# Hybrid encoder trunk: the second chunk of tokens prepared step by step in every group

## Chip, cores and metric

The kernel runs on one core of a Trainium2 chip. The metric is the device time of one execution in microseconds (us). Before the change it is 2895.91 us, the median of 3 runs (2895.25 to 2896.24).

## What is computed

One layer of a streaming encoder works on 2048 prompt tokens and on 8 x 16 sample tokens, with a model width of 1024:

```
h = RMSNorm(x);  p = h @ w_in            (1024 x 9216, split in column segments)
A: gated short convolution    B: gated linear recurrence, 4 heads    C: stick-breaking attention, 8 heads
y_x = o_x @ w_branch[rows of x]          for x in A, B, C
out = x + (sigmoid(m_a) y_a + sigmoid(m_b) y_b + sigmoid(m_c) y_c) @ w_out
```

Besides the result, the last rows of the convolution, the recurrent states and the keys and values are outputs.

## The kernel before, in words

The tokens are 17 tiles of 128 (tile 0 holds the sample tokens). `GROUPS` (L39) puts them into three groups of two chunks: [0,1,2] and [3,4]; [5,6,7] and [8,9,10]; [11,12,13] and [14,15,16]. For each group, `run_jobs` (L1317) walks over some 70 jobs. A job is one slice of weight columns, and a *turn* is one job on one chunk. `order` (L1327 to L1330) lists the turns of a group; in groups 1 and 2 it begins with (job 0, chunk 0), (job 1, chunk 0), (job 0, chunk 1), (job 1, chunk 1), numbered `at_` = 0 to 3. Jobs 0 and 1 of groups 1 and 2 are gate slices of the attention branch (`sz_job`, L1178): 24 matmuls of 128x384 each (`proj_chan`, L704, matmul at L710), with a `yield` after every 6. Products are made from split operands (high part and remainder), three passes each.

Between two yields of a turn, `run_jobs` issues other work: late post-processing, the recurrence (`hbg`), and background work (`bg`). The background work is the attention over the cached keys of the sample tokens in group 1, and the prompt attention (`attn_pair`, L297) in group 2 and in the merge stage behind it. The prompt attention begins in group 2's turn 0: it loads Q, K and V tiles (L281, L282, L287, L291), forms scores on TensorE (L329, L330), two sigmoids on ScalarE (L333, L335), masks on GpSimd (L338), a scan and a product on VectorE (L342, L347), and transposes on TensorE (L310) that a ScalarE copy evicts (L311).

`Prepare` (L585) turns x tiles into what the matmuls read, in steps:

- `load` (L598): a DMA of 512 KB into an `xt` tile (L607, on the SP queue), the sum of squares on ScalarE (L614), then two small operations on GpSimd (L232, L234).
- `scale` (L617): one operation on VectorE (L619).
- `turn` (L621), twice per tile: four transposes on TensorE (L629) into a PSUM tile `tp` (two buffers, shared with the attention and the sample attention), then a cast on ScalarE (L175) and a subtraction on VectorE (L176) into `hx`.

For groups 1 and 2 the order of the steps is written in `steps` (L633):

```
for i in range(n):
    for kk in range(0, KB, 4): self.turn(i, kk); yield
    for k in [i + 2] if self.final and i == 3 else [] if self.final and i == 2 else [i + 3]:
        if k < n: self.load(k); yield
    if i + 2 >= 3 and i + 2 < n: self.scale(i + 2); yield
    self.ready = i
```

There are three `xt` buffers: two in the pool `xp`, one in `xq`, and in the last group `xq` is used for tile index 2 alone (`room`, L602). So there the DMA of tile index 5 needs the buffer of index 3.

The next group's `Prepare` is begun in the last five turns of a group (L1350, L1359). `prep.chunk(ci)` (L687) runs all steps that are still missing until chunk `ci` is complete. It is called at each turn (L1348) for that turn's chunk. At the call for chunk 0 the generator stops behind the first `turn` of tile index 3; the others of chunk 1 are issued at once by the call of `at_` = 2. In group 1 these are six steps: turn(3,4), scale(5), turn(4,0), turn(4,4), turn(5,0), turn(5,4). In group 2 they are seven, with load(5) behind turn(3,4). In group 0 another list of steps (`first_steps`) is advanced in turns 0 and 1, two steps at each yield (L1356).

The framework that builds the kernel gives each engine its instruction order: it takes what is ready in its own model of time, and of that what stands first in the program. On the chip each engine then runs its list in that order.

Of the kernel before, what the change touches and what calls it, by code (L numbers as in the profile page):

```python
# [98 lines left out]
def trunk(ctx: ExitStack, tc: tile.TileContext, x_prompt, x_sample, cache_conv, state_hgrn, cache_k, cache_v,  # L99
# [88 lines left out]
    def wload(pieces, key):  # L188


        out = []
        for n, v in enumerate(pieces):
            a, b = v.shape[1], v.shape[2]
            if (key, n) in kept:
                turns[0] += 1
                if turns[0] % 4 == 0:

                    hl = []
                    for i in range(2):
                        x = wp.tile([P, a, b], F32, tag="wst", name="wst", bufs=2)  # L200
                        nc.sync.dma_start(x, kept[key, n][:, i].rearrange("p (a b) -> p a b", a=a).bitcast(F32))
                        hl.append(x.bitcast(F32R))
                    out.append((*hl, None))
                    continue
            w = wp.tile([P, 2, 1024], F32R, tag="w", name="w")
            hi, lo = (w[:, i].rearrange("p (a b) -> p a b", a=a) for i in range(2))
            if (key, n) in kept:
                nc.sync.dma_start(w.bitcast(F32), kept[key, n].bitcast(F32))
            else:
                st = wp.tile([P, a, b], F32, tag="wst", name="wst", bufs=2)  # L210
                nc.sync.dma_start(st, v)
                with ExitStack() as order:
                    if len(kept) < 1 and n:

                        for x in prep.last:
                            order.enter_context(tc.issue_after(x.ins))
                    split(hi, lo, st)
            out.append((hi, lo, w))
        return out
# [527 lines left out]
    def build_vectors():  # L747
        nc.sync.dma_start(qg_bc, q_norm_g[0].partition_broadcast(P))
        nc.sync.dma_start(kg_bc, k_norm_g[0].partition_broadcast(P))

        vrow = g0p.tile([17, P], F32, tag="mtmp", name="vrow", bufs=2)
        nc.sync.dma_start(vrow[0:12], conv_w[0].rearrange("j (b p) -> (j b) p", p=P))
        nc.sync.dma_start(vrow[12:16], hg_lb_logits[0].rearrange("(h p) -> h p", p=P))
        nc.sync.dma_start(vrow[16:17], hg_norm_g)
        pvec = ps_tp()
        nc.tensor.transpose(pvec[:, 0:17], vrow, idf[0:17, 0:17])
        nc.vector.tensor_copy(vec, pvec[:, 0:17])
# [10 lines left out]
    def build_bound():  # L768
        lmax = const.tile([P, 4], F32, name="lmax")
        nc.vector.tensor_copy(lmax, vec[:, 12:16])  # L770
        lexp = const.tile([P, 4], F32, name="lexp")
        nc.vector.tensor_tensor(lexp, vec[:, 12:16], lmax, ALU.subtract)
        ebase = const.tile([P, 1], F32, name="ebase")
        nc.vector.memset(ebase, 2.718281828459045)
        nc.gpsimd.tensor_tensor(lexp, ebase.broadcast_to([P, 4]), lexp, ALU.pow)
        lsum = const.tile([P, 4], F32, name="lsum")
        nc.vector.reciprocal(lsum, lexp)
        lsm = const.tile([P, 4], F32, name="lsm")
        nc.vector.tensor_tensor(lsm, lexp, lsum, ALU.mult)
        nc.vector.tensor_tensor(lb, lsm, lsm, ALU.subtract)  # L780
        nc.vector.tensor_scalar(omlb, lb, -1.0, 1.0, ALU.mult, ALU.add)
# [5 lines left out]
    def build_masks():  # L787
        for h in (1, 2, 4, 8, 16, 32, 64):
            nblk = 64 // h
            mt = g0p.tile([P, 2, 64], F32, tag="mtmp", name="mtmp", bufs=2)  # L790
            nc.gpsimd.memset(mt[:, :, :nblk], 1.0)
            for i in range(2):
                m = mt[:, i, :nblk]
                nc.gpsimd.affine_select(m, m, pattern=[[-2 * h, nblk]], base=-h * i, channel_multiplier=1,
                                        compare_op=ALU.is_ge, fill=0.0)
                nc.gpsimd.affine_select(m, m, pattern=[[2 * h, nblk]], base=h + h * i, channel_multiplier=-1,
                                        compare_op=ALU.is_gt, fill=0.0)
            lmask[h] = const.tile([P, 2 * nblk], I32, name=f"lmask{h}")
            nc.vector.tensor_copy(lmask[h].rearrange("p (i b) -> p i b", i=2), mt[:, :, :nblk])
# [4 lines left out]
    def build_rev():  # L804
        nc.gpsimd.memset(rev, 0.0)
        nc.gpsimd.affine_select(rev, rev, pattern=[[1, P]], base=1 - P, channel_multiplier=1,
                                compare_op=ALU.not_equal, fill=1.0)
# [39 lines left out]
    def build_hist():  # L847
        nc.gpsimd.memset(uhist, 0.0)
        nc.gpsimd.memset(shist, 0.0)
        nc.gpsimd.memset(cstage, 0.0)  # L850
        nc.sync.dma_start(cstage[0:16], cache_conv[0].rearrange("b t c -> (b t) c"))
# [101 lines left out]
    def build_selectors():  # L953
        nc.gpsimd.memset(qblk, 0.0)
        nc.gpsimd.memset(bsel, 1.0)
        nc.gpsimd.affine_select(bsel, bsel, pattern=[[-TS, NB]], base=0, channel_multiplier=1,
                                compare_op=ALU.is_ge, fill=0.0)
        nc.gpsimd.affine_select(bsel, bsel, pattern=[[TS, NB]], base=TS, channel_multiplier=-1,
                                compare_op=ALU.is_gt, fill=0.0)
# [299 lines left out]
    def run_late(cost):  # L1259
        for x in late:  # L1260
            x[0] -= cost
        for x in list(late):
            if x[0] <= 0:
                try:
                    x[0] = next(x[1])
                except StopIteration:
                    late.remove(x)
# [41 lines left out]
    def behind():  # L1309

        order = ExitStack()
        traced = nc.cur_bb.bb.instructions
        for engine in (nc.scalar, nc.vector, nc.sync):
            order.enter_context(tc.issue_after(next(i for i in reversed(traced) if i.engine == engine.engine)))
        return order

    def run_jobs(g, jobs):  # L1317
        nonlocal prep
        nxt = None
        n = len(jobs)  # L1320
        ws = {}

        def weights(i):
            if i < n and i not in ws:
                ws[i] = wload(*jobs[i][0])

        order = [(i, ci) for i in range(2, n - 2) for ci in range(2)]  # L1327
        begin = [(0, 0), (1, 0), (0, 1), (1, 1)] if g else [(0, 0), (0, 1), (1, 0), (1, 1)]
        order = (begin + order
                 + [(n - 2, 0), (n - 1, 0), (n - 2, 1), (n - 1, 1)])  # L1330
        for at_, (i, ci) in enumerate(order):
            weights(i)
            if g or at_:
                weights(i + 1)

            extra = g == 1 and 26 <= at_ < len(order) - 2 and jobs[i][2] == 1.0
            if not g and at_ == 0:
                prep.advance()
            if not g and at_ == 2:

                with tc.issue_after(rstd_at[0].ins), tc.issue_after(prep.last[1].ins):
                    build_vectors()
                    build_hist()
                    build_rev()
                    build_bound()
                    build_masks()
                    build_selectors()
            hT = prep.chunk(ci) if g or at_ > 1 else lambda ti, ci=ci: prep.tile(ci, ti)  # L1348
            left = len(order) - at_
            if left == 5 and g + 1 < len(GROUPS):  # L1350
                nxt = Prepare(g + 1)
            for turn_, cost in enumerate(jobs[i][1](ws[i], ci, hT)):
                if extra and turn_ == 1:
                    with behind():
                        next(splitting, None)
                if at_ < 2 and not g:  # L1356
                    prep.advance()
                    prep.advance()
                if nxt and (left <= 2 or nxt.ready < 0 and len(nxt.xt) < 3 or left <= 3 and not nxt.scaled):  # L1359
                    nxt.advance()  # L1360
                run_late(cost)
                hbg.run(cost * RATE_H)
                bg.run(cost * RATES[g] * jobs[i][2])
            if ci == 0 and g < len(GROUPS) - 1:
                wkeep(ws[i], jobs[i][0][1])
        while late:
            run_late(1e9)
        hbg.drain()
        prep = nxt
# [160 lines left out]
```

## Time and profile before

| | |
|---|---|
| median of 3 runs | 2895.91 us |
| the profiled execution | 2894.27 us |
| its span (first to last instruction) | 2892.5 us |
| TensorE (PE) busy | 2860.0 us, 99% of the span |
| VectorE (DVE), ScalarE (ACT), GpSimd (POOL) busy | 54%, 35%, 11% |
| mean granted TensorE clock, share of full | 0.998 |

The profile is of one execution. PE rows are matmuls, PEld rows are weight loads that overlap them, and SPq rows are DMA issues of the SP queue. In a timeline a row merges neighbouring instructions of one kind: its start, the time to the end of the last, the engine and line, what is written and read, the count, and in brackets the idle time of the engine before it with what ended it.

### The profile page before, as it was taken

How to read it: one execution, taken by the hardware profiler on the slowest of the kernel's cores; microseconds unless marked ns; L12 is line 12 of the kernel's file. 1: busy time of each engine (PE TensorE's matmuls, PEld its weight loads, DVE VectorE, ACT ScalarE, POOL GpSimd, SP SyncE). 2: the span in 40 equal slices, each digit the busy share in tenths (PEclk: the TensorE clock that was granted, in tenths of full speed). 3: DMA queues.
4: the chain of work that ended last, by engine and by line, in shares of the span. 5: the costliest groups of instructions: out<-in, count | busy, mean ns of one | idle time of the engine just before them, and what ended most of it. 6: DMA issues, size and time to landing. Idle time of an engine off the chain costs nothing.

```text
span 2892.5 us, 51725 instructions
## 1 busy us (share of the span) xinstructions
PE 2860.0 (99%) x19511; PEld 2668.9 (92%) x19511; DVE 1548.4 (54%) x3304; ACT 1023.7 (35%) x2391; POOL 315.9 (11%) x787
## 2 busy tenths in 40 slices
PE   9999999999999999998999999999999999999999
PEld 9999999989999999997999999999988888788888
DVE  5454645641344433545534757547475875867743
ACT  4333222242233332213334444434433444444420
POOL 3100000110100000001322111010010110010100
PEclk9999999999999999999999999999999999999999
DMA  8987767777678886755676453544446877778876
GB/s 306 312 261 240 242 219 246 244 226 241 206 237 271 271 271 221 245 160 164 210 233 204 142 179 128 163 137 152 146 139 222 296 237 235 262 250 263 273 257 217
DMA packets 367403, 645.57 MB, mean 223 GB/s; under 512 B 32969, under 2 KB 243746, under 8 KB 336434
## 3 DMA queue, kind: packets, MB, share of 16 engines
q1 hardware_dynamic: 367154, 642.26, 67.8%
q8 instruction: 155, 2.54, 0.4%
q14 instruction: 94, 0.77, 0.1%
HBM read 444.97 MB, written 197.17 MB: 222 GB/s over the span
## 4 chain that ended last, share of the span: by engine, by line
PE 77%; DVE 2%; DMA 1%; issue 0%; ACT 0%; SPq 0%; POOL 0%; DVEq 0%; ACTq 0%; POOLq 0%
PE acc L710 32%; PE acc L1438 10%; PE acc L721 9%; PE acc L1469 7%; PE pv L359 4%; PE tp L310 4%; PE z L330 2%; PE z L329 2%; PE z L1040 1%; PE tp L458 1%; PE pv L522 1%; DMA xt<-in_x_prompt_dram 0%; PE z L476 0%; PE hg L1087 0%; PE hg L827 0%
## 5 line engine op out<-in xcount | busy, mean ns | idle before, releaser
L710 PE MATMUL acc<-hx,w 128*128 128x384 f32 (+1 forms) x6816 | 1253.8, 333 | 2.0 <-DVE hx L176 1.3
L710 PEld LDWEIGHTS acc<-hx,w 128*128 128x128 f32 x6816 | 1107.3, 188 | 25.0 <-issue 15.2
L721 PE MATMUL acc<-w,hx 128*128 128x256 f32 x2544 | 329.0, 284 | 1.2 <-DVE hx L176 0.9
L342 DVE TENSOR_TENSOR_SCAN pr<-snb,carry 128x513 f32<-128x513 f32 x192 | 246.5, 1284 | 154.0 <-ACT snb L333 152.1
L721 PEld LDWEIGHTS acc<-w,hx 128*128 128x128 f32 x2544 | 311.3, 188 | 4.1 <-DVE hx L176 1.7
L311 ACT COPY aT<-tp 128x512 f32<-128x512 f32 (+2 forms) x320 | 167.5, 524 | 371.6 <-PE tp L310 358.8
L710 PE MATMUL acc<-hx,wst 128*128 128x384 f32 x1248 | 247.3, 344 | 0.0
L1438 PE MATMUL acc<-o,w 128*128 128x512 f32 (+2 forms) x1080 | 234.6, 363 | 1.0 <-DMA o<-OX 1.0
L333 ACT ACTIVATE snb<-z 128x512 f32<-128x512 f32 (+2 forms) x320 | 172.1, 538 | 143.7 <-PE z L330 140.2
L710 PEld LDWEIGHTS acc<-hx,wst 128*128 128x128 f32 x1248 | 215.5, 188 | 6.4 <-issue 3.7
L1438 PEld LDWEIGHTS acc<-o,w 128*128 128x128 f32 x1080 | 184.9, 188 | 32.9 <-issue 4.4
L347 DVE TENSOR_TENSOR sp<-sp,pr 128x512 f32<-128x512 f32 (+2 forms) x320 | 195.6, 611 | 31.8 <-POOL sp L338 5.2
L342 DVE TENSOR_TENSOR_SCAN pr<-snb,one 128x129 f32<-128x129 f32 (+3 forms) x128 | 114.7, 896 | 130.2 <-POOL snb L338 129.9
L310 PE MATMUL tp<-idf,sp 128*128 128x128 f32 x1088 | 171.4, 273 | 2.3 <-ACT aT L311 1.6
L335 ACT ACTIVATE sp<-z 128x512 f32<-128x512 f32 (+2 forms) x320 | 171.6, 536 | 0.0
L1469 PE MATMUL acc<-w,mh 128*128 128x256 f32 x816 | 160.5, 284 | 0.0
L310 PEld LDWEIGHTS tp<-idf,sp 128*128 128x128 f32 x1088 | 132.0, 141 | 19.4 <-issue 4.4
L1174 ACT ACTIVATE gm<-acc 128x384 f32<-128x384 f32 (+1 forms) x144 | 68.2, 474 | 229.4 <-PE acc L710 197.5
L176 DVE TENSOR_TENSOR w<-wst,w 128x1024 fp32r<-128x1024 f32 x72 | 88.1, 1223 | 105.8 <-ACT w L175 105.8
L1469 PEld LDWEIGHTS acc<-w,mh 128*128 128x128 f32 x816 | 130.7, 188 | 5.8 <-issue 4.2
L329 PE MATMUL z<-Kt,Q 128*128 128x512 f32 (+2 forms) x320 | 129.2, 404 | 0.2 <-ACT sp L335 0.2
L359 PE MATMUL pv<-aT,Vt 128*64 128x512 f32 (+3 forms) x640 | 128.1, 535 | 0.0
(302 smaller groups left out, 3575.8 us busy)
## 6 DMA issues: line engine op xcount, KB each, us to landing
w<-W SPq DMA_DIRECT2D x168, 1024.0 KB, 6.2
W<-w SPq DMA_DIRECT2D x72, 1024.0 KB, 5.0
wst<-W SPq DMA_DIRECT2D x112, 512.0 KB, 5.2
wst<-in_w_in_dram SPq DMA_DIRECT2D x72, 512.0 KB, 6.0
GM<-gm SPq DMA_DIRECT2D x120, 192.0 KB, 4.1
W<-mwp SPq DMA_DIRECT2D x40, 512.0 KB, 4.0
Kt<-KT SPq DMA_DIRECT2D x160, 128.0 KB, 3.6
o<-OX SPq DMA_DIRECT2D x72, 256.0 KB, 4.7
```

Source lines behind the costliest of these rows:

```text
L310: nc.tensor.transpose(tp[:, j * P:(j + 1) * P], sp[:, j * P:(j + 1) * P], idf)
L311: nc.scalar.copy(aT[:, e, 0:nb, i * P:(i + 1) * P], tp[:, :w].rearrange("p (b q) -> p b q", q=P))
L329: nc.tensor.matmul(z[:, :w], Q1[:, i * P:(i + 1) * P], Kt[:, :w], start=True, stop=False)
L333: nc.scalar.activation(sn[:, 512 - w:512], z[:, :w], AF.Sigmoid, scale=-0.125)
L335: nc.scalar.activation(sp[:, :w], z[:, :w], AF.Sigmoid, scale=0.125)
L342: nc.vector.tensor_tensor_scan(pr[:, 512 - w:513][:, ::-1], s_in, s_in, one if diag else carry[e][i], ALU.mult, ALU.bypass)
L347: nc.vector.tensor_tensor(sp[:, :w], sp[:, :w], pr[:, 513 - w:513], ALU.mult)
L359: nc.tensor.matmul(pv[64 * e:64 * e + 64, c0:n], Vt[:, j, e], aT[:, e, j, c0:n], start=first and j == 0, stop=last and j == nb - 1, skip_g ...
L710: nc.tensor.matmul(acc[:, :n], w[0][a][:, k], hT[b][:, k, :n], start=k == 0 and i == 0, stop=k == KB - 1 and i == 2)
L721: nc.tensor.matmul(acc[:, :256], hT[b][:, k, ti * P:(ti + 1) * P], w[k // 4][a][:, k % 4], start=k == 0 and i == 0, stop=k == KB - 1 and i ...
L1438: nc.tensor.matmul(acc[:, :n], w[0][a][:, k, dd * P:(dd + 1) * P], box[x][b][:, k, sl], start=k == 0 and i == 0, stop=k == 3 and i == 2)
L1469: nc.tensor.matmul(acc[:, :256], box["l" if b else "h"][:, k, ti * P:(ti + 1) * P], w[k // 4][a][:, k % 4], start=k == 0 and i == 0, stop= ...
```

## The change

In the first two turns of a group, `prep.advance()` is called twice at every yield, in all groups instead of group 0 alone. Each call issues one step of `Prepare`. The call stands ahead of the background work of the same yield.

```
@@ -1353,7 +1353,7 @@
                 if extra and turn_ == 1:
                     with behind():
                         next(splitting, None)
-                if at_ < 2 and not g:
+                if at_ < 2:
                     prep.advance()
                     prep.advance()
                 if nxt and (left <= 2 or nxt.ready < 0 and len(nxt.xt) < 3 or left <= 3 and not nxt.scaled):
```

## Rows read from the trace of the kernel before

**Rows 1.** Stretches of the span: length, busy time of each engine, granted clock, DMA.

```profile
590.00:625.00 35.00, 31.63 (x226) 29.81 (x227) 17.66 (x27) 17.00 (x35) 5.02 (x13) 1.00 0.73 236
625.00:1330.00 705.00, 705.00 (x5260) 685.49 (x5259) 278.85 (x783) 200.28 (x523) 40.82 (x80) 1.00 0.71 231
1330.00:1380.00 50.00, 35.68 (x209) 32.94 (x208) 23.64 (x39) 19.79 (x48) 10.48 (x24) 0.86 0.60 180
1380.00:1950.00 570.00, 570.00 (x3807) 538.03 (x3806) 305.01 (x644) 224.06 (x570) 108.55 (x242) 1.00 0.54 174
```

**Rows 2.** Waits of PE, whole span: total us, times, longest us.

```profile
PE tp L629 <- DVE xt L619: 11.7, 3, 9.5
PE tp L629 <- DVE hx L176: 4.6, 2, 3.6
```

**Rows 3.** Timeline of PE at the start of group 2.

```profile
1339.67 7.63 PE L710 MATMUL acc<-hx,w 128*128 128x384 f32 x42
...
1350.20 1.19 PE L629 MATMUL tp<-idf,xt 128*128 128x128 f32 x8
...
1351.40 0.33 PE L329 MATMUL z<-Kt,Q 128*128 128x256 f32 x1
1355.36 0.66 PE L629 MATMUL tp<-idf,xt 128*128 128x128 f32 x4 [3.63 <-DVE hx L176]
...
1365.98 1.94 PE L629 MATMUL tp<-idf,xt 128*128 128x128 f32 x8 [9.49 <-DVE xt L619]
1367.74 2.69 PE L710 MATMUL acc<-hx,w 128*128 128x384 f32 x7
1370.23 0.42 PE L310 MATMUL tp<-idf,sp 128*128 128x128 f32 x2
```

**Rows 4.** A short stretch of the same place, columns as in rows 1.

```profile
1369.00:1370.00 1.00, 1.00 (x5) 1.00 (x4) 0.27 (x1) 0.00 (x0) 0.00 (x0) 0.50 0.00 0
```

**Rows 5.** Timeline of all engines there: load and scale of tile index 5.

```profile
1357.53 0.38 SPq L607 DMA_DIRECT2D xt<-in_x_prompt_dram  x1
1362.46 1.06 ACT L614 ACTIVATE junk<-xt 128x1024 bf16<-128x1024 f32 x1 [5.15 <-DMA xt<-in_x_prompt_dram]
...
1364.55 1.28 DVE L619 SCALAR_TENSOR_TENSOR xt<-xt,rr,g_bc 128x1024 f32<-128x1024 f32 x1 [5.34 <-POOL rr L234]
...
1367.72 0.69 DVE L176 TENSOR_TENSOR hx<-tp,hx 128x512 fp32r<-128x512 f32 x1 [1.89 <-ACT hx L175]
```

**Rows 6.** The same timeline: scale of index 4, SP queue at the group's start.

```profile
1339.88 0.51 SPq L281 DMA_DIRECT2D Q<-QT  x1
...
1342.54 1.29 DVE L619 SCALAR_TENSOR_TENSOR xt<-xt,rr,g_bc 128x1024 f32<-128x1024 f32 x1 [1.24 <-POOL rr L234]
...
1348.07 0.53 SPq L1183 DMA_DIRECT2D SZ<-gm  x1
```

**Rows 7.** Timeline of PE at the start of group 1.

```profile
601.93 1.03 PE L629 MATMUL tp<-idf,xt 128*128 128x128 f32 x8
603.93 1.25 PE L629 MATMUL tp<-idf,xt 128*128 128x128 f32 x8 [0.96 <-DVE hx L176]
605.86 0.45 PE L710 MATMUL acc<-hx,w 128*128 128x384 f32 x1 [0.68 <-ACT hx L175]
...
610.89 1.15 PE L710 MATMUL acc<-hx,w 128*128 128x384 f32 x5 [1.30 <-DVE hx L176]
```

**Rows 8.** Timeline, group 1's start: first matmul, scale of index 5, scale for group 2.

```profile
591.44 0.42 PE L710 MATMUL acc<-hx,w 128*128 128x384 f32 x1
...
598.22 1.28 DVE L619 SCALAR_TENSOR_TENSOR xt<-xt,rr,g_bc 128x1024 f32<-128x1024 f32 x1 [1.83 <-POOL rr L234]
...
608.95 1.28 DVE L619 SCALAR_TENSOR_TENSOR xt<-xt,rr,g_bc 128x1024 f32<-128x1024 f32 x1 [2.42 <-POOL rr L234]
```

**Rows 9.** The page's costliest groups: the attention's scan and product on DVE.

```profile
L347 DVE TENSOR_TENSOR sp<-sp,pr 128x512 f32<-128x512 f32 (+2 forms) x320 | 195.6, 611 | 31.8 <-POOL sp L338 5.2
L342 DVE TENSOR_TENSOR_SCAN pr<-snb,one 128x129 f32<-128x129 f32 (+3 forms) x128 | 114.7, 896 | 130.2 <-POOL snb L338 129.9
```

More of the change, by code (lines that the diff above doesn't have):

```diff
@@ L1355, in run_jobs @@
                         next(splitting, None)
-                if at_ < 2 and not g:
+                if at_ < 2:
                     prep.advance()
```

## Prediction

> **What bounds the kernel now.** I read the span in stretches first, then the waits of PE, then the timeline where these waits lie. The stretches show PE busy without a gap for most of the time: 705 of 705 us in the body of group 1, 570 of 570 us behind the start of group 2 [rows 1]. Two short stretches stand out, and both are where a group begins: 3.4 us without PE in 590 to 625, and 14.3 us in 1330 to 1380, where the granted clock is also down to 0.86 [rows 1]. So PE sets the time, and a microsecond that PE gains at those places should reach the end, since no later stretch has a gap in which it could get lost. The list of waits says what PE stands for there: the transposes of the preparation (L629) wait 11.7 us for the scaled tile and 4.6 us for the split that frees their PSUM buffer, both of them longest in one single wait (9.5 and 3.6 us) [rows 2].
>
> The timeline of group 2 shows these waits one after another. Turns 0 and 1 run through (42 matmuls in 7.63 us, so 0.18 us each). Then come the eight transposes of turn(3,4) and turn(4,0), a wait of 3.63 us, turn(4,4), a wait of 9.49 us, the last eight transposes, and only then turn 2 [rows 3]. The long wait is the chain of tile index 5: its DMA is issued at 1357.53, ScalarE takes the landed tile at 1362.46, VectorE scales it at 1364.55, and PE goes on at 1365.98, so 8.45 us from issue to transposes [rows 3, 5]. It could not be issued earlier, because its buffer is free only after turn(3,4). The wait also costs clock: it is granted at half (the 1.2 GHz level) still at 1369 to 1370, three microseconds after PE resumed [rows 4]: the seven matmuls there take 2.69 us [rows 3] instead of 7 x 0.18 = 1.3. In group 1 the same burst costs less, since its tile 5 is loaded and scaled long before (598.22 [rows 8]): idle times of 0.96, 0.68 and 1.30 us, together 2.9 us [rows 7].
>
> **What can be won.** In group 2, from the end of the last score matmul ahead of the waits (1351.40 + 0.33 = 1351.73) to 1370.23 [rows 3] there are 18.5 us. The work in them is 12 transposes at 0.13 (eight in 1.03 us [rows 7]) = 1.6, seven matmuls = 1.3, and three score matmuls, at 0.18 too = 0.5: 3.4 us. So 15.1 us are lost in group 2, idle time and slow clock together, and 2.9 us in group 1: 18.0 us at most.
>
> **The change, step by step.** Nothing is added or removed; six steps in group 1 and seven in group 2 are issued earlier in the program. At two a yield they are through after three yields of turn 0 in group 1 and four in group 2, so all of them lie in the first turn, not in two, and `chunk(1)` at turn 2 finds nothing to do. Group 0 keeps its code.
>
> *PE.* The 20 transposes of each group (2.6 us) are done in either kernel. Now they stand between matmuls of turns 0 and 1, whose 48 x 0.18 = 8.6 us cover what they wait for. That cover is the whole gain.
>
> *SP and the DMA (group 2).* The load of tile 5 is issued in turn 0's first yield. It needs turn(3,4), which follows six matmuls: 1339.67 + 1.1 + 0.5 = 1341.3. SP is then in the middle of issuing the attention's first tiles, thirteen of them back to back from 1339.88 to 1348.07 [rows 6], 0.6 us each; these are later in the program, so the load should take the next place, near 1341.9. If the load stands in the queue before its buffer is free, it holds the attention's loads for about the same 1.5 us; those feed background work, and PE has matmuls left.
>
> *Chain.* 1341.9 + 8.45 = 1350.4 for the transposes of tile 5. From the first of them to the first matmul of turn 2 it took 1.8 us before (1365.98 to 1367.74 [rows 3]), so turn 2 can start at 1352.2. PE itself gets there at 1339.67 + 8.6 + 2.6 for 20 transposes + 1.4 for the eight score matmuls that stood there before = 1352.3. The two times meet, so the wait is between nothing and a few microseconds.
>
> *ScalarE and VectorE.* Five casts, five subtractions and one scale move forward into turns 0 and 1; in group 2 also one sum of squares with the two small GpSimd operations behind it, on which only this scale waits. Tile 4 is scaled at 1342.54 + 1.29 = 1343.8 [rows 6], in time for the first yields. From 1348 on both engines also have the attention's first units, which can hold a cast or a subtraction for one operation (a scan and a product have means of 0.9 and 0.6 us [rows 9]). For this, and for an order of the streams that was made for other times, I leave 3 us lost in group 2; the bounds are 0 and the 8.1 of the rival on stream order below. A wait that short should not bring the clock down.
>
> *Group 1.* Tile 5 is scaled at 598.22 + 1.28 = 599.5 [rows 8]. PE starts turn 0 at 591.44 and has 48 matmuls and 20 transposes, 11.2 us, to 602.6 without counting the sample attention. So the last transposes, cast and subtraction (1.8 us) fit ahead of turn 2. No DMA of group 1 moves, but the buffers that come free earlier let the first tiles of group 2 be loaded earlier too. That already happens here: one of them is scaled at 608.95, after VectorE waited 2.42 us for it [rows 8], and the subtraction behind it is what PE waits 1.30 us for [rows 7]. The same delay will fall into turn 0 or 1, where PE has matmuls left. I leave 1 us lost, from bounds of 0 and 2.8 (below).
>
> **Sum.** Group 2: 15.1 - 3 = 12.1. Group 1: 2.9 - 1 = 1.9. Together 14.0 us off. The profiled execution took 2894.27 us (a span of 2892.5 and 1.8 us around it), which becomes 2880.3. The median of the runs is 1.6 us above the profiled one, so 2882 us for the median.
>
> **Rivals.**
>
> *The load comes behind the attention's loads.* If SP's order places it behind those thirteen transfers, which run until 1348.07 [rows 6], the chain ends at 1348.1 + 8.45 = 1356.5 against PE's 1352.3: a wait of about 4.2 us, and up to 1.4 us for a fallen clock (the seven matmuls above). Group 2 then wins about 9.5, with group 1's 1.9 some 11.4 us: 2884.5. For it: the load cannot go before turn(3,4). Against: it stands first in the program among what is ready.
>
> *The streams take the steps as literally as the program has them.* PE then comes to tile 5's transposes after 18 matmuls and 12 transposes, at 1339.67 + 3.2 + 1.6 = 1344.5, and waits until 1350.4: 5.9 us, and with the clock as it fell before [rows 4] up to 2.2 more. In group 1 the same point is 591.44 + 4.8 = 596.2, but with the key transposes of the sample attention nearer 596.7, against 599.5: 2.8 us. Group 2 wins 7.0, group 1 0.1: 2888.8. The engine queues speak for it: ScalarE ran nothing for 5.15 us while its next instruction waited for the DMA [rows 5]. The Trainium skill states this as a rule in TensorE: Matmul & The Clock Gate, section "Architectural detail": the queues of ScalarE and VectorE are strictly first in, first out; by that rule, with which the trace agrees here, everything behind a step that comes too early waits with it. Against: the order is made from readiness, and before the change PE put matmuls ahead of transposes that were not ready.
>
> *Slower: the attention's first units take over the wait.* Until now the two long waits gave VectorE and ScalarE time to finish them. Should PE meet each of the first eight transposed units (four query tiles, two heads) before VectorE has made it, it pays scan and product, 8 x (0.90 + 0.61) = 12.1 us [rows 9], on top of the 5.9 + 2.2 + 2.8 = 10.9 us of the literal order: 23.0 against 18.0 that are won, so 2901, and with the moved scale (1.28) and five subtractions (0.69 each [rows 5]) in the same queue 2906. It decides where these new waits pass 18.0 us. Against it: VectorE is busy for only 23.6 of the 50 us [rows 1], and the matmuls of turns 2 and 3 stand between the units.
>
> *No gain.* Waits of the same size return elsewhere at the groups' starts, because the two scarce PSUM buffers of the transposes are shared with the attention: 2896.
>
> **Chances.** 0.2%, or 5.8 us, is about what a measurement of this kernel can tell from no change; the bounds are 2890.1 and 2901.7. The forecast has 0.60, the late load 0.15, the literal order 0.10 (a little of it beyond 2890), no gain 0.09, slower 0.06. Faster by more than 0.2%: 0.84, within 0.2%: 0.10, slower: 0.06. The range goes from all 18.0 us won, with 1 us for the clock's and pipeline's refilling in group 1 that the idle times do not show (2877), to the upper end of the literal order (2890).
>
> **What would show it.** In the changed profile: no transposes of L629 in one block ahead of turn 2 in groups 1 and 2; the DMA of L607 within about 3 us of group 2's first matmul rather than 18; the waits of L629 down from 16.3 us to a few; the granted clock 1.00 through 1330 to 1380. A wait of more than 8 us on L629, L310 or L710 within turns 0 to 3 would prove the forecast wrong, and so would new PE gaps in the body of group 1 or 2, where there are none now.

## The result, and the profile after

The changed kernel takes 2880.89 us, the median of 4 runs (2877.70 to 2881.77), against 2896.07 us for the kernel before, also 4 runs. The ratio is 0.9943 with a 95% interval of 0.9926 to 0.9961: 15.2 us or 0.5% faster by the medians. The forecast was 2882 us.

The profiled execution after took 2877.70 us (span 2875.8), against 2894.27 (2892.5) before. It is the fastest of its four runs, so the two profiles stand 16.6 us apart, a little more than the medians. One experiment below was run twice, because its first profiled execution had a granted clock of 0.75; nothing is read from that execution, its time included.

The stretches of the changed kernel, to be held against [rows 1] (the later ones begin about 10 and 15 us earlier, as the work does; columns as there):

```profile
590.00:625.00 35.00, 34.59 (x255) 32.85 (x254) 17.55 (x28) 17.29 (x37) 7.95 (x16) 1.00 0.70 233
625.00:1320.00 695.00, 695.00 (x5183) 675.48 (x5182) 275.69 (x775) 197.68 (x514) 38.77 (x77) 1.00 0.71 233
1320.00:1370.00 50.00, 47.17 (x316) 44.86 (x316) 28.13 (x49) 23.80 (x60) 13.24 (x30) 1.00 0.71 210
1370.00:1935.00 565.00, 565.00 (x3760) 533.08 (x3759) 304.86 (x647) 223.06 (x564) 106.32 (x237) 1.00 0.55 175
```

PE is missing 0.4 us at the start of group 1 (3.4 before) and 2.8 us at the start of group 2 (14.3 before), the clock is at 1.00 in both, and the long bodies still have no gap. The waits of PE over the whole span, columns as in [rows 2]:

```profile
PE tp L629 <- DVE xt L619: 3.4, 4, 1.6
PE tp L1113 <- DVE hx L176: 2.4, 2, 1.4
PE tp L310 <- ACT aT L311: 1.6, 1, 1.6
```

The waits of L629 have gone from 16.3 us to 3.4, and 2.3 us of these lie in group 0. The next waits in the list were in the kernel before as well. At the start of group 2, PE's timeline has the steps among the matmuls (compare [rows 3]):

```profile
1335.82 1.29 PE L710 MATMUL acc<-hx,w 128*128 128x384 f32 x6
1336.98 0.63 PE L629 MATMUL tp<-idf,xt 128*128 128x128 f32 x4
1337.36 2.36 PE L710 MATMUL acc<-hx,w 128*128 128x384 f32 x12
1340.13 0.63 PE L629 MATMUL tp<-idf,xt 128*128 128x128 f32 x4 [0.41 <-DVE xt L619]
...
1345.81 0.74 PE L629 MATMUL tp<-idf,xt 128*128 128x128 f32 x5 [0.74 <-DVE xt L619]
...
1349.48 0.30 PE L310 MATMUL tp<-idf,sp 128*128 128x128 f32 x1 [0.57 <-DVE sp L347]
...
1361.37 1.58 PE L721 MATMUL acc<-w,hx 128*128 128x256 f32 x12
```

The long wait is now 0.74 us, and its clock loss is gone. The timeline of all engines shows why, in the chain of tile index 5 (compare [rows 5]):

```profile
1337.64 0.33 SPq L607 DMA_DIRECT2D xt<-in_x_prompt_dram  x1
...
1342.28 1.06 ACT L614 ACTIVATE junk<-xt 128x1024 bf16<-128x1024 f32 x1 [0.28 <-DMA xt<-in_x_prompt_dram]
...
1344.38 1.28 DVE L619 SCALAR_TENSOR_TENSOR xt<-xt,rr,g_bc 128x1024 f32<-128x1024 f32 x1 [1.66 <-POOL rr L234]
```

The load is issued 1.8 us behind group 2's first matmul (1337.64 - 1335.82) instead of 17.9 (1357.53 [rows 5] - 1339.67 [rows 3]). From issue to transposes it takes 8.2 us, against 8.45 before. The chain is as long as it was and now lies beside matmuls.

Two stretches of PE's timeline locate the gain, and they are used for all experiments. *Group 1's start* goes from the first 384-column matmul to the first transposes of L499, a fixed point in the sample attention behind it; *group 2's start* goes from its first matmul to the first matmul of L721 (turn 4). Before they took 26.3 and 39.3 us; after, 23.5 and 25.6. That is 2.8 + 13.7 = 16.5 us. The other differences between the two profiles (1.1 us less ahead of group 1, 0.9 us more behind the start of group 2) lie in code that the change leaves alone. They nearly cancel, which is luck.

### The profile page after: what moved, and what is told of

Read it like the earlier page. It is cut to its first block, busy times and chain, and to the rows that moved or that the text cites. A ratio compares the mean times of both kernels' runs of the same rounds, so it can differ in the third digit from the quotient of the medians.

```text
span 2875.8 us, 51728 instructions
## 1 busy us (share of the span) xinstructions
PE 2857.6 (99%) x19511; PEld 2666.8 (93%) x19511; DVE 1548.3 (54%) x3304; ACT 1024.3 (36%) x2391; POOL 317.6 (11%) x787
## 4 chain that ended last, share of the span: by engine, by line
PE 76%; DVE 2%; DMA 2%; issue 1%; ACT 0%; POOL 0%; SPq 0%; DVEq 0%; POOLq 0%; ACTq 0%
PE acc L710 32%; PE acc L721 10%; PE acc L1438 9%; PE acc L1469 7%; PE pv L359 4%; PE tp L310 4%; PE z L330 2%; PE z L329 2%; PE z L1040 1%; PE tp L458 1%; DMA gate<-GM 1%; PE pv L522 1%; PE z L476 0%; PE hg L1087 0%; PE hg L827 0%
## 5 line engine op out<-in xcount | busy, mean ns | idle before, releaser
L710 PEld LDWEIGHTS acc<-hx,w 128*128 128x128 f32 x6816 | 1106.5, 188 | 22.1 <-issue 15.2
L721 PE MATMUL acc<-w,hx 128*128 128x256 f32 x2544 | 329.2, 284 | 1.0 <-DVE hx L176 0.7
L721 PEld LDWEIGHTS acc<-w,hx 128*128 128x128 f32 x2544 | 311.4, 188 | 3.9 <-DVE hx L176 1.6
L1438 PE MATMUL acc<-o,w 128*128 128x512 f32 (+2 forms) x1080 | 234.7, 363 | 1.2 <-DMA o<-OX 1.2
L1438 PEld LDWEIGHTS acc<-o,w 128*128 128x128 f32 x1080 | 185.0, 188 | 33.2 <-issue 4.7
L347 DVE TENSOR_TENSOR sp<-sp,pr 128x512 f32<-128x512 f32 (+2 forms) x320 | 195.5, 611 | 25.6
L310 PE MATMUL tp<-idf,sp 128*128 128x128 f32 x1088 | 171.3, 273 | 2.6 <-ACT aT L311 1.6
L310 PEld LDWEIGHTS tp<-idf,sp 128*128 128x128 f32 x1088 | 131.9, 141 | 19.6 <-issue 4.4
```

Source lines behind the costliest of these rows:

```text
L310: nc.tensor.transpose(tp[:, j * P:(j + 1) * P], sp[:, j * P:(j + 1) * P], idf)
L347: nc.vector.tensor_tensor(sp[:, :w], sp[:, :w], pr[:, 513 - w:513], ALU.mult)
L710: nc.tensor.matmul(acc[:, :n], w[0][a][:, k], hT[b][:, k, :n], start=k == 0 and i == 0, stop=k == KB - 1 and i == 2)
L721: nc.tensor.matmul(acc[:, :256], hT[b][:, k, ti * P:(ti + 1) * P], w[k // 4][a][:, k % 4], start=k == 0 and i == 0, stop=k == KB - 1 and i ...
L1438: nc.tensor.matmul(acc[:, :n], w[0][a][:, k, dd * P:(dd + 1) * P], box[x][b][:, k, sl], start=k == 0 and i == 0, stop=k == 3 and i == 2)
```

## The experiments

Each kernel was timed in turn with the kernel before. "Ratio" is to that, with its 95% interval. The kernel before took 2896.07 to 2898.89 us beside the different kernels, so gains are to be compared rather than times. A ratio comes from all runs of a kernel, a stretch from its one profiled execution.

| kernel | group 1's start, us | group 2's start, us | ratio |
|---|---|---|---|
| before | 26.3 | 39.3 | 1 |
| the change | 23.5 | 25.6 | 0.9943 (0.9926 to 0.9961) |
| group 1 alone | 23.5 | 40.1 | 0.9988 (0.9978 to 0.9997) |
| group 2 alone | 26.3 | 26.2 | 0.9947 (0.9932 to 0.9962) |
| load alone | 27.4 | 29.7 | 0.9968 (0.9955 to 0.9981) |
| all but the load | 26.9 | 39.8 | 0.9999 (0.9989 to 1.0009) |
| the same, load by ScalarE's queue | 25.9 | 28.1 | 0.9960 (0.9946 to 0.9974) |
| behind the background work | 24.0 | 31.4 | 0.9960 (0.9946 to 0.9974) |
| one step a yield | 23.7 | 30.9 | 0.9954 (0.9939 to 0.9969) |
| turn 1 alone | 23.8 | 36.1 | 0.9979 (0.9969 to 0.9988) |
| steps held in place | 30.2 | 31.3 | 0.9973 (0.9963 to 0.9983) |

Stretches of code that an edit leaves alone differ from profile to profile: group 1's start takes 25.9 to 27.4 us, group 2's 39.3 to 40.1, and what lies behind group 2's start 1513.1 to 1517.5 us. There, at L1438, PE waits for a DMA for 0.95 us in the kernel before, 1.23 in the changed one and 2.11 in "behind the background work".

**One group at a time.** For group 1 alone, and with `g != 1` in place of `g < 2` for group 2 alone:

```
-                if at_ < 2 and not g:
+                if at_ < 2 and g < 2:
```

> The early steps in group 1 alone (group 2 as before). Two stretches of PE's timeline are compared: group 1's start, from the first 384-column matmul of its turn 0 to the first transposes of L499 (26.3 us in the kernel before, 23.5 after), and group 2's start, from its first matmul of turn 0 to the first matmul of L721 (39.3 before, 25.6 after). Theory (each group saves what PE stood for at its own start): 23.5 and 39.3 us, time 2.8 us below before, near 2893. Rival (the gain is a changed order of later work, or differs from run to run): other stretches change too and the time is not that of the parts.

> The early steps in group 2 alone (group 1 as before). Theory (each group saves its own waits): group 1's start 26.3 us, group 2's start 25.6 us, time 13.7 us below before, near 2882. Rival (order of later work): the two single-group kernels do not add up to the whole change.

Measured: 2894.36 and 2882.41 us, against 2898.22 for the kernel before, timed beside them. The two stretches move where the steps move (group 2's 40.1 instead of 39.3 differs by less than group 1's start does among kernels that leave it alone), and the two ratios, 0.12% and 0.53% off, add up to 0.65%, within the interval of the whole change (0.39% to 0.74%). Each group saves its own waits; group 2 has most of it. Nothing speaks for the rival, a changed order of later work: what lies behind group 2's start takes 1513.6 and 1514.9 us in these kernels, not less than the 1513.6 before.

**The load alone, and all but the load.** In the first kernel only two steps of group 2 are issued early (this edit and the next are against the kernel before):

```
-                if at_ < 2 and not g:
+                if at_ < 2 and not g or g == 2 and at_ == 0 and turn_ == 0:
                     prep.advance()
                     prep.advance()
```

> In group 2 only turn(3,4) and load(5) are issued in the first yield of turn 0, all other steps in one block ahead of turn 2 as before; group 1 as before. Theory (most of the gain is the chain behind the load of tile 5): the long wait of 9.5 us and the 2.2 us of half clock behind it go, the 3.6 us wait for VectorE stays, so group 2's start takes 27 to 29.5 us and the time is some 11 us below before, near 2885. Rival (the block of transposes with its two PSUM buffers is what costs): 36 us or more, near 2893.

In the second, load(5) and scale(5) are put behind turn(4,4), and the three steps ahead of them are issued early:

```
-                for k in [i + 2] if self.final and i == 3 else [] if self.final and i == 2 else [i + 3]:
+                for k in [i + 1] if self.final and i == 4 else [] if self.final and i in (2, 3) else [i + 3]:
                     if k < n:
                         self.load(k)
                         yield
-                if i + 2 >= 3 and i + 2 < n:
-                    self.scale(i + 2)
+                k = 5 if self.final and i == 4 else 6 if self.final and i == 3 else i + 2
+                if 3 <= k < n:
+                    self.scale(k)
...
+                if g == 2 and at_ == 0 and turn_ < 3:
+                    prep.advance()
```

> The counterpart: in group 2 turn(3,4), turn(4,0) and turn(4,4) are issued in the first three yields of turn 0, while load(5) and scale(5) come behind turn(4,4) and so stay in the block ahead of turn 2; group 1 as before. Theory (the load's chain): the 3.6 us wait for VectorE goes, a wait of about 9 us for the scaled tile and its half clock stay; group 2's start 34 to 37 us, near 2892. Rival (the block of transposes): below 30 us, near 2885.

The load alone brings 9.6 us of the 13.7 (39.3 to 29.7, a little above the range given), and 2888.70 us is 9.5 us below the kernel before beside it. What stays is waits of the block, the longest for VectorE, which has the attention's first units ahead of the split (timelines of PE and of VectorE in that kernel):

```profile
1357.65 0.44 PE L629 MATMUL tp<-idf,xt 128*128 128x128 f32 x2 [2.90 <-DVE hx L176]
```

```profile
1353.72 2.21 DVE L342 TENSOR_TENSOR_SCAN pr<-snb,one 128x385 f32<-128x385 f32 x2
1355.86 1.13 DVE L347 TENSOR_TENSOR sp<-sp,pr 128x384 f32<-128x384 f32 x2
1356.91 1.27 DVE L176 TENSOR_TENSOR hx<-tp,hx 128x512 fp32r<-128x512 f32 x2
```

Behind this wait the granted clock was 0.50 from 1359 to 1362.

All but the load brings nothing: 39.8 us and a ratio of 0.9999, outside the expectation of 34 to 37. Its transposes are among the matmuls as they should be, and the time comes back whole at tile 5 (timeline of all engines):

```profile
1341.06 0.63 PE L629 MATMUL tp<-idf,xt 128*128 128x128 f32 x4
...
1344.83 0.60 PE L629 MATMUL tp<-idf,xt 128*128 128x128 f32 x4
...
1358.74 0.41 SPq L607 DMA_DIRECT2D xt<-in_x_prompt_dram  x1
...
1363.71 1.06 ACT L614 ACTIVATE junk<-xt 128x1024 bf16<-128x1024 f32 x1 [9.10 <-DMA xt<-in_x_prompt_dram]
...
1367.23 1.94 PE L629 MATMUL tp<-idf,xt 128*128 128x128 f32 x8 [13.54 <-DVE xt L619]
```

One wait of 13.54 us stands where 3.63 and 9.49 stood [rows 3]. So the 3.6 us were in the shadow of the load: PE spent them while SP had not yet issued it. The row of SP says more. Tile index 3, whose buffer the load takes, is through its transposes at 1341.7, but the load goes out 17 us later. The buffer was not what it waited for. In the kernel before it was not the last thing either: there turn(3,4) is over by 1351.4 [rows 3], and the load goes out at 1357.53 [rows 5], at least 6.1 us later. SP's own waits in that kernel, between 1340 and 1360, say what its list stood on:

```profile
SPq L320 <- DMA wst<-W: 1.8, 1, 1.8
...
SPq L291 <- DMA wst<-W: 1.0, 1, 1.0
```

and in the kernel before, between 1350 and 1360:

```profile
SPq L320 <- DMA wst<-W: 2.3, 1, 2.3
```

SP takes about 0.6 us per issue, has twenty-five of them from the group's first matmul to the load, and also stands still until earlier weight loads have landed, by the releaser that the profile names.

**The same load by another queue.** To tell SP's list from the place of the step, the kernel without the early load got one more edit:

```
-            nc.sync.dma_start(xt, x_tile(self.tiles[i][2]))
+            q = nc.scalar if self.final and i == 5 else nc.sync
+            q.dma_start(xt, x_tile(self.tiles[i][2]))
```

> The kernel that left load(5) and scale(5) in the block ahead of turn 2, with one difference: the DMA of tile 5 in the last group goes out by ScalarE's queue instead of SP's. Theory (what delayed tile 5 is its place in SP's list behind the attention's loads, not the buffer and not the place of the step in the program): the DMA is issued right behind turn(3,4), some 2 to 3 us after group 2's first matmul instead of 18.9, the wait of 13.5 us for the scaled tile goes, group 2's start takes 26 to 29 us, time 2882 to 2886. Rival (a step issued ahead of turn 2 is late on any queue): group 2's start stays at 37 us or more, 2895 or above.

Measured: 28.1 us and 2885.38 us (lines are numbered one to two higher in this kernel):

```profile
1339.72 0.63 PE L630 MATMUL tp<-idf,xt 128*128 128x128 f32 x4
...
1340.39 0.37 ACTq L608 DMA_DIRECT2D xt<-in_x_prompt_dram  x1
...
1348.12 0.33 PE L329 MATMUL z<-Kt,Q 128*128 128x128 f32 x1 [1.38 <-DMA Q<-QT]
...
1353.09 1.03 PE L630 MATMUL tp<-idf,xt 128*128 128x128 f32 x8
...
1355.89 0.44 PE L712 MATMUL acc<-hx,w 128*128 128x384 f32 x1 [1.08 <-DVE gm L1136]
```

The step stands at the same late place in the program, but the load goes out 1.8 us behind the first matmul (1338.55) and the wait for the tile is gone; moving one DMA to another queue wins 11.7 us at this place (39.8 to 28.1). Of the 2.5 us to the changed kernel some 2 are PE's waits, 3.8 us against 1.7; the longest are 1.38 us for an attention tile and, right behind the last transposes, 1.08 us for VectorE's gate product (L1136).

**Where the calls stand, and how many.** With the two calls behind the background work of the yield (against the kernel before; group 0 keeps its calls):

```
                 bg.run(cost * RATES[g] * jobs[i][2])
+                if at_ < 2 and g:
+                    prep.advance()
+                    prep.advance()
```

> Two steps a yield in turns 0 and 1 of groups 1 and 2 as in the changed kernel, but the calls stand behind the background work of the yield instead of ahead of it. In the SP queue the load of tile 5 then follows the attention's first thirteen loads. Theory (where SP issues the load decides): it is issued some 8.4 us behind group 2's first matmul instead of 1.8, the transposes of tile 5 can begin at 16.9 us, PE reaches them at 12.5, so a wait of about 4.4 us, group 2's start 29 to 31 us against 25.6, time about 4 us above the changed kernel. Rival (the matmuls of turns 0 and 1 cover the chain anyway): no wait above 1.5 us, stretch 25 to 26.5 us.

With one call instead of two in groups 1 and 2, run twice (against the changed kernel):

```
                 if at_ < 2:
                     prep.advance()
-                    prep.advance()
+                    if not g:
+                        prep.advance()
```

> One step a yield instead of two in turns 0 and 1 of groups 1 and 2, so that the steps do spread over two turns. Theory: turn(3,4) is now alone in the first yield and load(5) comes in the second, behind the background work of the first; SP issues it behind the attention's thirteen loads, and a wait of 4 to 6 us for tile 5 comes back: group 2's start 29 to 32 us, 3 to 6 us above the changed kernel. Group 1 as in the changed kernel, 23 to 24 us. Rival (a gentler spread leaves ScalarE and VectorE more room): stretch at or below 25.6 us.

> One step a yield in turns 0 and 1 of groups 1 and 2, a second time for a readable profile. Theory (SP's list decides): tile 5 is loaded behind the attention's thirteen loads, as where the calls stood behind the background work; a wait of 4 to 6 us and group 2's start 29 to 32 us, against 25.6 with two steps a yield; group 1's start 23 to 24 us. Rival (a gentler spread is as good): at or below 26 us.

Measured: 2886.50 us for the first; 2885.37 and 2885.65 us for the second. Both let the load fall behind the attention's thirteen loads, and both pay for it. One step a yield:

```profile
1338.64 0.63 PE L629 MATMUL tp<-idf,xt 128*128 128x128 f32 x4
...
1345.88 0.53 SPq L607 DMA_DIRECT2D xt<-in_x_prompt_dram  x1
...
1354.76 1.94 PE L629 MATMUL tp<-idf,xt 128*128 128x128 f32 x8 [5.25 <-DVE xt L619]
```

Behind the background work, the same; the stretch of 31.4 us is a little above the range given:

```profile
1346.71 0.53 SPq L607 DMA_DIRECT2D xt<-in_x_prompt_dram  x1
...
1356.16 1.94 PE L629 MATMUL tp<-idf,xt 128*128 128x128 f32 x8 [5.29 <-DVE xt L619]
```

The load goes out 8.4 us behind the first matmul of group 2, as expected, instead of 1.8; the wait is 5.3 us (4.4 expected), and some 4.5 us at half clock follow (0.50 from 1356.0 to 1360.5, behind the background work). Spreading the steps more gently is worse here: two calls ahead of the background work put load(5) into the same yield as turn(3,4), one call does not.

**Turn 1 alone.** Against the changed kernel:

```
-                if at_ < 2:
+                if at_ < 2 and not g or g and at_ == 1:
```

> The steps of groups 1 and 2 are issued in turn 1 alone, none in turn 0, so half of the matmuls stand ahead of them. Theory: the load of tile 5 comes behind the attention's first loads and two weight loads, about 10 us behind group 2's first matmul; a wait of about 6 us for tile 5, group 2's start 30 to 33 us; group 1, whose tiles are loaded before, keeps most of its gain (24 to 25 us). Time near 2887. Rival (one turn is cover enough): below 27 us, 2881 to 2882.

Measured: 2890.97 us, group 1's start 23.8 us as expected, group 2's 36.1 us, outside the range of 30 to 33:

```profile
1345.58 0.96 SPq L201 DMA_DIRECT2D wst<-W  x2
...
1346.63 0.38 SPq L607 DMA_DIRECT2D xt<-in_x_prompt_dram  x1
...
1355.13 1.06 ACT L614 ACTIVATE junk<-xt 128x1024 bf16<-128x1024 f32 x1 [5.90 <-DMA xt<-in_x_prompt_dram]
1357.22 1.28 DVE L619 SCALAR_TENSOR_TENSOR xt<-xt,rr,g_bc 128x1024 f32<-128x1024 f32 x1 [4.39 <-POOL rr L234]
1358.66 1.09 PE L629 MATMUL tp<-idf,xt 128*128 128x128 f32 x4 [9.99 <-DVE xt L619]
```

The place in SP's list was right (10.0 us behind the first matmul). The landing was not: ScalarE got the tile 8.5 us after the issue, where the other kernels took 4.5 to 5.3 by SP's queue (6.2 by ScalarE's). The load had gone out right behind two weight loads of 512 KB each; where such a pair went out behind it (one step a yield), the tile took 5.2 us. That these shared the DMA engines with it is the likely cause, and was not tried by itself.

**The steps held where the program has them.** In groups 1 and 2, everything that PE does behind a step in turns 0 and 1 is ordered behind that step's transposes (against the changed kernel):

```
+        held_ = ExitStack()
...
+                    if g and at_ == 0:
+                        held_.close()
+                        traced = nc.cur_bb.bb.instructions
+                        held_.enter_context(tc.issue_after(
+                            next(x for x in reversed(traced) if x.engine == nc.tensor.engine)))
...
+            if at_ == 1:
+                held_.close()
```

> The changed kernel, but everything that TensorE does in turns 0 and 1 of groups 1 and 2 behind a step is held behind that step's transposes, so that its list has the steps where the program has them. Theory (the gain needs the freedom to put matmuls ahead of transposes that are not ready): PE comes to tile 5's transposes after 18 matmuls and waits about 5 us there in group 2, with or without half clock behind it, and about 2.8 us in group 1: stretches of 30 to 34 us and 25 to 27 us, 2886 to 2890. Rival (the cover is large enough in any order): 25.6 and 23.5 us, 2881.

Measured: 2889.07 us. In group 2, waits of 1.44 and 4.04 us for scaled tiles, stretch 31.3 us, as expected. Group 1 took 30.2 us, above its range of 25 to 27, although its wait is only 3.00 us (PE's timeline, then stretches of it):

```profile
589.16 0.44 PE L1113 MATMUL tp<-idf,on 128*128 128x128 f32 x2 [1.76 <-DVE hx L176]
...
597.83 1.94 PE L629 MATMUL tp<-idf,xt 128*128 128x128 f32 x8 [3.00 <-DVE xt L619]
599.43 2.27 PE L710 MATMUL acc<-hx,w 128*128 128x384 f32 x6
```

```profile
586.00:592.00 6.00, 4.24 (x28) 3.86 (x27) 3.89 (x7) 2.91 (x8) 0.75 (x2) 0.85 0.78 285
592.00:596.00 4.00, 2.83 (x13) 2.41 (x12) 1.54 (x3) 2.43 (x5) 0.38 (x2) 0.80 0.89 273
596.00:600.00 4.00, 2.17 (x10) 2.20 (x11) 2.88 (x3) 1.40 (x4) 1.94 (x3) 0.63 0.74 297
600.00:604.00 4.00, 4.00 (x19) 3.68 (x17) 0.98 (x2) 1.54 (x3) 0.00 (x0) 0.52 0.11 27
```

The clock is at half there, and six matmuls take 2.27 us where they take 1.29 in the changed kernel. Not all of this is the edit's: the clock was down twice, from 597.8 to 603.9 behind the wait of 3.00 us, and before that from 590.4 to 593.7, behind the wait of 1.76 us at L1113, which stands ahead of the first held step. The kernel "load alone", whose group 1 is that of the kernel before, also fell to half behind this wait (1.86 us there, 0.50 from 591 to 594); the kernel before did not (1.71 us, 1.00). The profiled execution (2892.03 us) is also the slowest of eight, 3 us above their median, so what group 1 loses in the other executions stays open. Group 2 and the ratio carry the conclusion: the stretch is 5.7 us longer than in the changed kernel, and about half of the gain is gone (0.9973 against 0.9943). So the steps being earlier in the program is not enough: the gain also needs the freedom to put matmuls ahead of transposes that are not ready.

## Why the prediction was right, point by point

- *PE is the bound and the waits at the groups' starts reach the end.* Right in the main. The stretches saved 16.5 us and the spans differ by 16.7; that they agree so well is in part luck, since 0.9 us was lost behind group 2's start and 1.1 us gained ahead of group 1. "No later stretch has a gap" rests on rows that end at 1950 [rows 1]: PE's wait at L1438 lies behind them.
- *What can be won, 18.0 us.* 16.5 of it came, 13.7 of 15.1 in group 2 and 2.8 of 2.9 in group 1. The 1 us that the lower end of the range adds for refilling in group 1 shows in no run; the clock there was at 1.00 before the change too [rows 1].
- *The residue, 3 us and 1 us.* Too careful in both: PE's waits left at group 2's start are 0.41, 0.74 and 0.57 us; at group 1's start one of 0.4 us is left, on the sample attention's transposes (L458). These two terms are nearly all of the difference between 14.0 and the 16.6 of the profiles; by the medians 15.2 us came off. "A wait that short should not bring the clock down" was not put to the test, since no such wait was left; in "load alone" one of 2.90 us was followed by half clock.
- *SP's place and the chain.* Right: issue 1.8 us behind the first matmul (2.2 predicted), then 8.2 us (8.45). That two calls ahead of the background work decide this was in the text only as "it stands first in the program"; the experiments show how much hangs on it.
- *"It could not be issued earlier, because its buffer is free only after turn(3,4)".* This step of the reading was wrong as the cause of the late load, and rows 3 and 5 already speak against it: the load goes out at least 6.1 us after turn(3,4). With turn(3,4) early and the step left late, it still went out 18.9 us behind the first matmul, and by ScalarE's queue 1.8 us. SP's list held it back. The sum did not suffer, since the change moves both the transposes and the load's place in the list.
- *The 3.63 us as a term beside the 9.49.* They add up on PE's timeline, but not as gains: taken away alone, the first is worth nothing, because the load is issued no earlier. The load alone was worth 9.6 us, the rest 4.1 more only with it.
- *The rivals' prices.* The late load was priced at a gain of 11.4 us; the two kernels that have it gain 11.6 and 13.3 us by their ratios and wait 5.3 us instead of 4.2. The literal order was priced at 7.1 us and gains 7.8 by its ratio. Its group 2 comes near the price (8.0 us saved instead of 7.0, waits of 5.5 us instead of 5.9). In group 1, priced at 0.1, the one profiled execution loses 3.9 us against the kernel before, most of it to the clock.
- *The slower rival.* The attention's transposes (L310) wait 0.57 us at one place. It did not occur.

## What to carry to other kernels

Steps that are moved as a block have a few instructions that carry the gain; here one DMA of 512 KB, by where it stands in its queue's list. Before spreading work over more slots, see which of its transfers falls behind whose: here one step a slot instead of two put the load behind thirteen others and cost some 5 us at that place. And two waits that follow each other on the bound engine are worth their sum only if neither is in the shadow of the other's cause.

## What the runs showed of the hardware that was not expected

- The SP queue stood still within its list: in "all but the load" for 1.8 us and 1.0 us until a weight load had landed, by the releaser that the profile names. The waiting issues move attention tiles and no weights; what they wait for in truth is not shown.
- The 512 KB load of tile 5 landed after 4.6 us (changed kernel) or 4.9 us (kernel before); right behind two loads of the same size ScalarE took it 8.5 us after the issue. The Trainium skill, DMA: Bandwidth & Descriptors, section "Anatomy of one DMA", gives about 2.0 us plus the bytes at 436 GB/s for the GpSimd path, an estimate of 3.2 us for this size; the loads of tiles here went by SP's queue, from 3.6 us to landing (the fastest, in the changed kernel) to 9.1 (the slowest, in the kernel before), and the measured times decide.
- The length of one wait did not settle the granted clock. Waits of 0.4 to 0.7 us in the changed kernel left it at 1.00. Behind 2.90 us ("load alone") it was at 0.50 from 1359 to 1362, but behind 3.63 us in the kernel before it was still at 1.00 from 1355 to 1356. At the same code ahead of group 1, 1.71 us left it at 1.00 (kernel before) and 1.86 us were followed by 0.50 from 591 to 594 ("load alone").
